# One trunk layer on one core: the first FFN blocks in passes, with their low parts and T sums on VectorE moved

## The chip, the cores and the metric

The kernel runs on one core of a Trainium2 chip. The metric is the device time of one launch in microseconds (us). The core has TensorE for matrix products, VectorE and ScalarE for elementwise work, GpSimd, and SyncE (SP), which issues most loads. Each engine works through its own queue in order, and an instruction that waits holds up everything behind it on its engine.

## The reference

The layer takes x of 512 tokens by 1024 features, all float32:

```
h  = LN(x) * (1 + scale1(c)) + shift1(c)
x1 = LN_1(alpha * x + gate1(c) * HybridMixer(h))          # attention and mLSTM branches, then w_out
h2 = LN(x1) * (1 + scale2(c)) + shift2(c)
out = LN_2(alpha * x1 + gate2(c) * SwiGLU(h2))
SwiGLU(h) = (silu(h @ w_gate) * (h @ w_up)) @ w_down      # 2816 hidden features
```

The change lies between HybridMixer's output projection (w_out), the two normalisations that make h2 from it, and the first of the 22 hidden blocks of 128 features of SwiGLU.

## The kernel before, in words

**Split numbers.** Every matrix operand is kept as a rounded high part and a low part (the value less its high part). The high part is a cast on ScalarE (line 154 for weights, line 178 for activations), the low part a subtraction on VectorE (lines 155 and 179). A product is three matmuls: high by high, high by low, low by high (`mm3`, lines 168 to 175, whose three matmuls have the lines 171, 174 and 175). `POOL_LO` (line 94) names the weights whose low part is subtracted by GpSimd instead: the first piece of the kernel, and the gate and up weights of the FFN blocks 0 and 1.

**Weights.** `emit_chunk` (line 142) loads a weight into a `raw` buffer (a ring of 3; the last two pieces of w_out use the two buffers of the conditioning pool, tag `adaw`), casts it to `whi` and subtracts it to `wlo` (rings of 4). The weights of FFN block 2 go to buffers of their own (`fh`, `fl` in the profile), in the place of two pieces of w_out.

**Output projection and normalisation.** The 512 tokens are 4 tiles of 128. For a tile `wo_seg` makes two halves of 512 features, each 8 slices (`lo4` and `hi4` are the first and last four); `resid1` (line 768) adds the residual and collects statistics; `ln1_a` (line 793) does the first normalisation in place (lines 795, 796) and the second as `xh` (line 799, ScalarE). Each normalisation needs a power -0.5 of the variance, which GpSimd computes (line 195, `lnrs`), and xh a bias (`nmr`, line 200, VectorE). `ln1_b` (line 802) transposes xh on TensorE (8 transposes, line 810, `h2t`), scales it into `h32` (line 815 on ScalarE; for the last tile ScalarE writes the high part and VectorE h32, line 817) and splits it into `hhi` and `hlo` (lines 178 and 179; line 820 for the last tile). The h32 buffers are a ring of 3.

**First FFN blocks.** Blocks 0, 1 and 2 are computed directly: for the first 256 tokens (tiles 0 and 1) gate then up of a block, 8 slices of three matmuls each (lines 911 to 918), with the transposes of tile 2 behind block 0 and those of tile 3 after four slices of block 2; then for the last 256 tokens (lines 923 to 925). The first matmul of each gate or up product is pinned: it stays behind the instruction that the program has before it on TensorE.

**T sums.** The other 19 blocks use seven products in place of eight, with sums of quarter matrices. `build_t` (line 828) makes four sums per pair of tiles from h32 (lines 834 to 837) and splits them into `thi` and `tlo` (lines 839, 840). Its buffers `tt` come from the `raw` ring. `load_pair` (line 897) loads the weights of a block with their sums: one load of 512 KB and three of 256 KB on SP, and two of 256 KB on GpSimd's queue that are added onto what is there (lines 907, 908).

**What sets the order.** A planner fixes the order on each engine when the kernel is built: among instructions that it takes to be ready, the one earlier in the program goes first, and those in a `tc.high_priority()` block go ahead of others. `after(ins, prev)` adds an order edge on one engine, `tc.keep_in_program_order` pins as described. Buffers of a closed pool are reused by the next one once their last reader is done.

Of the kernel before, what the change touches and what calls it, by code (L numbers as in the profile page):

```python
# [16 lines left out]
P = 128  # L17
D = 1024
S = 512
KT = 8  # L20
# [12 lines left out]
CW = 1056  # L33
# [57 lines left out]


PLAN = plan()
POOL_LO = [("start", 0), ("fg", 0), ("fu", 0), ("fg", 1), ("fu", 1)]


@with_exitstack
def block_kernel(ctx, tc, x, c, wada, wpk, cols, gvb, mvb, lnp, out):
    nc = tc.nc
    V, A, G, T = nc.vector, nc.scalar, nc.gpsimd, nc.tensor  # L100
# [26 lines left out]
    stp = ctx.enter_context(tc.tile_pool(name="stp", bufs=4))  # L127
# [5 lines left out]
    st = {"n": 0, "tiles": {}, "resident": {}}  # L133
# [8 lines left out]
    def emit_chunk(i):  # L142
        key = PLAN[i]
        w = chunk_width(key)
        if key in (("wo", 6), ("wo", 7)):
            raw = adap.tile([P, VW], F32, tag="adaw", name=f"raw{i}", bufs=2)
        else:
            raw = stp.tile([P, CW], F32, tag="raw", name=f"raw{i}", bufs=3)
        st["dma"] = nc.sync.dma_start(raw[:, :w], wpk[offs[key]:offs[key] + P * w].rearrange("(p w) -> p w", p=P))
        if key in st["resident"]:  # L150
            hi, lo = st["resident"][key]
        else:
            hi, lo = (stp.tile([P, CS], F32R, tag=t_, name=f"{t_}{i}")[:, w_off(key):w_off(key) + w] for t_ in ("whi", "wlo"))
        st["hi"] = A.copy(hi[:, :w], raw[:, :w])  # L154
        (G if key in POOL_LO else V).tensor_tensor(lo[:, :w], raw[:, :w], hi[:, :w].bitcast(F32), ALU.subtract)  # L155
        st["tiles"][key] = (hi, lo)

    def prefetch(key, ahead):
        i = PLAN.index(key)
# [4 lines left out]
    def get(key, ahead=AHEAD):  # L164
        prefetch(key, ahead)
        return st["tiles"].pop(key)
# [17 lines left out]
    def ln_stats(src):  # L184
        stt = small.tile([P, 2, 6], F32, tag="lnst", name="lnst")
        for h in range(2):
            V.bn_stats(stt[:, h, :], src[:, h * 512:(h + 1) * 512])
        return stt

    def ln_finish(stt):  # L190
# [6 lines left out]

    def nmr(mu_, rs):
        t = small.tile([P, 1], F32, tag="nmr", name="nmr")
        V.tensor_scalar(t, mu_, rs, -1.0, ALU.mult, ALU.mult)  # L200
        return t

    def after(ins, prev):
        tc.add_manual_dep(ins.ins, prev.ins.name, mybir.DependencyInfo(mybir.DependencyClass.NoSync, mybir.DependencyReason.DATA), reason="issue order")
        return ins

    def scope(**kw):
        e = ExitStack()
# [33 lines left out]
    ada_s, adap = scope(name="ada", bufs=2)  # L242
# [83 lines left out]
    for tb in range(TB):  # L326
# [3 lines left out]
        rs = small.tile([P, 1], F32, tag="lnrs", name=f"xrs{tb}")  # L330
# [47 lines left out]
    def hk(k, sl=slice(0, S)):  # L378
        return hhi[:, k, sl], hlo[:, k, sl]
# [330 lines left out]
    for f in range(KT):  # L710
# [4 lines left out]
        hi, lo = get(("pa", f))  # L715
# [21 lines left out]
    for i, c0 in ((0, 16), (1, 40)):  # L737
        pg = tr_tile(f"pg{i}")
# [11 lines left out]
    ln_s, lnq = scope(name="lnq", bufs=1, side="right")  # L750
# [42 lines left out]
    def ln1_a(tb):  # L793
        mu_, rs = ln_finish(zst[tb])
        V.scalar_tensor_tensor(xz[tb], xz[tb], mu_, l1g, ALU.subtract, ALU.mult)
        V.scalar_tensor_tensor(xz[tb], xz[tb], rs, l1b, ALU.mult, ALU.add)
        mu_, rs = ln_finish(ln_stats(xz[tb]))
        xh = lnq.tile([P, D], F32, tag="xh", name=f"xh{tb}")
        A.activation(xh, xz[tb], AF.Identity, bias=nmr(mu_, rs), scale=rs)
        xhs[tb] = xh  # L800

    def ln1_b(tb):
        xh = xhs.pop(tb)
        ts_ = slice(tb * P, (tb + 1) * P)
        h32 = lnq.tile([P, KT, P], F32, tag="h32", name=f"h32{tb}", bufs=3)
        h32s[tb] = h32
        for g in range(2):
            pt = tr_tile(f"h2t{tb}{g}")
            for i in range(4):
                T.transpose(pt[:, i * P:(i + 1) * P], xh[:, (g * 4 + i) * P:(g * 4 + i + 1) * P], ident)  # L810
            for i in range(4):
                d = g * 4 + i
                s_ = slice(i * P, (i + 1) * P)
                sh, sc = mods[:, 32 + d:33 + d], sc2p[:, d:d + 1]
                A.activation(h32[:, d, :] if tb < TB - 1 else hhi[:, d, ts_], pt[:, s_], AF.Identity, bias=sh, scale=sc)
                if tb == TB - 1:
                    V.tensor_scalar(h32[:, d, :], pt[:, s_], sc, sh, ALU.mult, ALU.add)
            if tb == TB - 1:
                ds_ = slice(g * 4, g * 4 + 4)
                V.tensor_tensor(hlo[:, ds_, ts_], h32[:, ds_, :], hhi[:, ds_, ts_].bitcast(F32), ALU.subtract)  # L820
        if tb < TB - 1:
            split(hhi[:, :, ts_], hlo[:, :, ts_], h32)

# [4 lines left out]
    def build_t(a, b):  # L828
        ts_ = slice(a * P, (a + 1) * P)
        b11, b21 = h32s[a][:, 0:4, :], h32s[a][:, 4:8, :]  # L830
        b12, b22 = h32s[b][:, 0:4, :], h32s[b][:, 4:8, :]
        tt = [stp.tile([P, CW], F32, tag="raw", name=f"tt{i}_{a}", bufs=3) for i in range(2)]
        t = [tt[i // 2][:, (i % 2) * S:(i % 2) * S + S].rearrange("p (k t) -> p k t", k=4) for i in range(4)]
        V.tensor_tensor(t[0], b11, b12, ALU.subtract)
        V.scalar_tensor_tensor(t[1], b22, -1.0, t[0], ALU.mult, ALU.subtract)
        V.tensor_tensor(t[2], b22, b12, ALU.subtract)
        V.scalar_tensor_tensor(t[3], b21, -1.0, t[1], ALU.mult, ALU.subtract)
        for i in range(4):
            A.copy(thi[:, i, :, ts_], t[i])
            V.tensor_tensor(tlo[:, i, :, ts_], t[i], thi[:, i, :, ts_].bitcast(F32), ALU.subtract)  # L840

    lo4, hi4, all8 = range(4), range(4, KT), range(KT)
# [20 lines left out]
    ln1_b(1)  # L863
    wo_seg(1, 3, lo4)
    NF0 = 3
    first = []
    for k, key in enumerate((("fg", 2), ("fu", 2))):
        st["resident"][key] = tuple(lnq.tile([P, D], F32R, tag=f"wr{n}{4 + k}", name=f"f{n}{k}") for n in ("h", "l"))
    for f in range(NF0):
        with tc.high_priority():  # L870
            w_ = get(("fg", f), ahead=0), get(("fu", f), ahead=0)
        first.append((*w_, acc2(f"fg{f}"), acc2(f"fu{f}")))
    wo_seg(0, 3, hi4)
    resid1(3, 0, wops[(0, 3)])
    wo_seg(1, 3, hi4)
    resid1(3, 1, wops[(1, 3)])
    ln1_a(3)

    def ffn_mm(ps, w, sl, pin=False, ks_=range(KT)):
        hi, lo = w  # L880
        for k in ks_:
            s_ = slice(k * P, (k + 1) * P)
            mm3(ps[:, sl], (hi[:, s_], lo[:, s_]), hk(k, sl), k == 0, k == KT - 1, pin and k == ks_[0])

    y_s.close()
    ada_s.close()
    tp_s, tp = scope(name="tp", bufs=1)
    thi = tp.tile([P, 4, 4, 256], F32R, name="thi")
    tlo = tp.tile([P, 4, 4, 256], F32R, name="tlo")

    raws = {}

# [4 lines left out]
    def load_pair(f):  # L897
        if f >= FT:
            return
        g = stp.tile([P, CW], F32, tag="raw", name=f"rawg{f}", bufs=3)[:, 0:D]  # L900
        nc.sync.dma_start(g, wpk[offs[("fg", f)]:offs[("fg", f)] + P * D].rearrange("(p w) -> p w", p=P))
        w = tp.tile([P, 3 * S], F32, tag="raw", name=f"raws{f}", bufs=2)
        s1, s3, u2 = (w[:, i * S:(i + 1) * S] for i in range(3))
        for d in (s1, s3):
            nc.sync.dma_start(d, chunk("fu", f, 0))
        nc.sync.dma_start(u2, chunk("fu", f, 1))
        nc.gpsimd.dma_start(s1, chunk("fu", f, 1), accum_op=ALU.add)
        nc.gpsimd.dma_start(s3, chunk("fg", f, 0), accum_op=ALU.add)
        raws[f] = (g, w)

    for f, (wg, wu, pg, pu) in enumerate(first):
        ffn_mm(pg, wg, slice(0, 256), True, lo4)
        if f == 2:
            ln1_b(3)
        ffn_mm(pg, wg, slice(0, 256), True, hi4)
        ffn_mm(pu, wu, slice(0, 256), True)
        if f == 0:
            ln1_b(2)
    build_t(0, 2)
    build_t(1, 3)  # L920
    load_pair(NF0)
    load_pair(NF0 + 1)
    for wg, wu, pg, pu in first:
        ffn_mm(pg, wg, slice(256, 512))
        ffn_mm(pu, wu, slice(256, 512))
# [10 lines left out]
    for f, (_, _, pg, pu) in enumerate(first):  # L936
        t = ftp.tile([P, 7, 256], F32, tag="r", name=f"at{f}", bufs=1).rearrange("p a t -> p (a t)")[:, 0:S]
# [119 lines left out]
    for q in range(4):  # L1057
        pss = [acc2(f"dn{q}{tb}") for tb in range(TB)]
        kl = FT if q < 3 else 8
        for k in range(kl):  # L1060
            if k % 4 == 0:
                w = get(("dn", q * 6 + k // 4))
# [111 lines left out]
```

## Time and profile before

| | us |
|---|---|
| median of 3 runs | 879.7 (879.41 to 880.75) |
| profiled execution | 874.97 |
| its span, first to last instruction | 873.2 |
| TensorE busy in the span | 837.4 (96%) |
| VectorE busy | 597.6 (68%) |
| ScalarE busy | 381.8 (44%) |
| GpSimd busy | 91.8 (11%) |

The profile shows one execution. PE is TensorE's matmuls, PEld its weight loads, DVE VectorE, ACT ScalarE, POOL GpSimd, SP the load queue. Times in rows are from the span's start. A matmul's row shows its own duration; matmuls overlap, so the distance between two starts is what one costs.

### The profile page before, as it was taken

To read this page: it belongs to the slowest core of one execution; us is meant where nothing else is said; L and a number is where in the kernel's file an instruction comes from. 1 tells how busy PE (TensorE), PEld (TensorE's weight loads), DVE (VectorE), ACT (ScalarE), POOL (GpSimd) and SP (SyncE) were. 2 spreads that over 40 slices of the span, in tenths; PEclk is the share of its full clock that TensorE was granted. 3 is DMA by queue.
4 is the path that set the end of the run, shared out by engine and by line. 5 is a ranking of instruction groups with operands and counts; after the bars stand their busy time and mean duration, and the time that the engine had idled before them with its cause. 6 is when DMAs were issued, how large, how long until landed. Compare 5 with 4: busy or idle time off the path is not lost.

```text
span 873.2 us, 14109 instructions
## 1 busy us (share of the span) xinstructions
PE 837.4 (96%) x5510; PEld 750.0 (86%) x5510; DVE 597.6 (68%) x1106; ACT 381.8 (44%) x605; POOL 91.8 (11%) x147
## 2 busy tenths in 40 slices
PE   5999999999989999999999987899999999999996
PEld 3889878777779888888888877899999999999996
DVE  6977546564497658766667796598878887943347
ACT  5555857674454324322222554444444444612110
POOL 4020000000111110000000260012111110000001
PEclk9999999999999999999999998999999999999999
DMA  8962432521221226767784072377777774542212
GB/s 336 350 176 73 141 103 69 138 72 61 97 75 47 90 68 230 259 233 248 261 294 151 1 193 73 102 193 189 179 195 182 171 188 101 173 128 87 98 37 97
DMA packets 46477, 130.08 MB, mean 149 GB/s; under 512 B 5293, under 2 KB 5693, under 8 KB 46410
## 3 DMA queue, kind: packets, MB, share of 16 engines
q1 hardware_dynamic: 37930, 113.97, 38.8%
q0 software_dynamic: 6752, 12.06, 8.1%
q10 hardware_dynamic: 1728, 3.15, 1.2%
q8 instruction: 43, 0.70, 0.3%
q14 instruction: 24, 0.20, 0.1%
HBM read 124.93 MB, written 2.13 MB: 146 GB/s over the span
## 4 chain that ended last, share of the span: by engine, by line
PE 89%; DVE 3%; ACT 1%; issue 1%; DVEq 0%; POOL 0%; ACTq 0%; POOLq 0%
PE p L171 7%; PE p L175 7%; PE p L174 7%; PE dn L171 5%; PE dn L174 5%; PE dn L175 5%; PE mv L171 2%; PE mv L175 2%; PE mv L174 2%; PE mo L171 2%; PE mo L174 2%; PE ga L175 2%; PE gb L175 2%; PE pb L175 2%; PE ga L174 2%; PE gb L171 2%
## 5 line engine op out<-in xcount | busy, mean ns | idle before, releaser
L155 DVE TENSOR_TENSOR wlo<-raw,whi 128x1024 fp32r<-128x1024 f32 (+3 forms) x101 | 112.8, 1120 | 109.7 <-ACT whi L154 102.6
L154 ACT CAST whi<-raw 128x1024 fp32r<-128x1024 f32 (+3 forms) x106 | 102.1, 968 | 183.5 <-PE dn L175 69.1
L174 PE MATMUL dn<-wlo,ah 128*128 128x256 f32 x352 | 96.7, 276 | 0.0
L171 PE MATMUL dn<-whi,ah 128*128 128x256 f32 x352 | 96.6, 276 | 0.0
L175 PE MATMUL dn<-whi,al 128*128 128x256 f32 x352 | 95.5, 276 | 0.0
L171 PE MATMUL p<-thi,whiu 128*128 128x256 f32 x304 | 85.3, 280 | 0.0
L174 PE MATMUL p<-tlo,whiu 128*128 128x256 f32 x304 | 84.9, 279 | 0.0
L175 PE MATMUL p<-thi,wlou 128*128 128x256 f32 x304 | 84.8, 279 | 0.0
L171 PE MATMUL p<-hhi,whiu 128*128 128x256 f32 x228 | 64.5, 283 | 2.8 <-DVE at L939 2.8
L171 PEld LDWEIGHTS dn<-whi,ah 128*128 128x128 f32 x352 | 66.0, 188 | 0.2 <-ACT ah L178 0.2
L174 PEld LDWEIGHTS dn<-wlo,ah 128*128 128x128 f32 x352 | 66.1, 188 | 0.0
L175 PEld LDWEIGHTS dn<-whi,al 128*128 128x128 f32 x352 | 65.3, 188 | 0.0
L174 PE MATMUL p<-hlo,whiu 128*128 128x256 f32 x228 | 64.3, 282 | 0.0
L175 PE MATMUL p<-hhi,wlou 128*128 128x256 f32 x228 | 64.3, 282 | 0.0
L254 DVE CUSTOM_DVE_ANT_0 adaw<-adaw,cb 128x1024 f32<-128x1024 f32 x32 | 39.1, 1223 | 27.6 <-DMA adaw<-in_wada_dram 27.5
L171 PEld LDWEIGHTS p<-thi,whiu 128*128 128x128 f32 x304 | 57.2, 188 | 0.0
L175 PEld LDWEIGHTS p<-thi,wlou 128*128 128x128 f32 x304 | 57.2, 188 | 0.0
L174 PEld LDWEIGHTS p<-tlo,whiu 128*128 128x128 f32 x304 | 57.0, 187 | 0.0
L195 POOL TENSOR_TENSOR lnrs<-lnrs,mhalf 128x1 f32<-128x1 f32 x12 | 12.1, 1007 | 322.4 <-DVE lnrs L194 322.4
L171 PEld LDWEIGHTS p<-hhi,whiu 128*128 128x128 f32 x228 | 43.4, 190 | 3.0 <-issue 3.0
L178 ACT CAST whiu<-raws 128x1024 fp32r<-128x1024 f32 (+1 forms) x38 | 30.8, 834 | 34.1 <-PE p L174 33.9
L175 PEld LDWEIGHTS p<-hhi,wlou 128*128 128x128 f32 x228 | 43.6, 191 | 0.0
(335 smaller groups left out, 2380.4 us busy)
## 6 DMA issues: line engine op xcount, KB each, us to landing
raw<-in_wpk_dram SPq DMA_DIRECT2D x84, 512.0 KB, 3.6
adaw<-in_wada_dram SPq DMA_DIRECT2D x48, 512.0 KB, 4.8
raws<-in_wpk_dram SPq DMA_DIRECT2D x57, 256.0 KB, 3.7
raws<-in_wpk_dram POOLq DMA_DIRECT2D x38, 256.0 KB, 6.4
rawg<-in_wpk_dram SPq DMA_DIRECT2D x19, 512.0 KB, 4.3
raw<-in_wpk_dram SPq DMA_DIRECT2D x16, 256.0 KB, 2.7
raw<-in_wpk_dram SPq DMA_DIRECT2D x8, 384.0 KB, 4.7
raw<-in_wpk_dram SPq DMA_DIRECT2D x4, 528.0 KB, 5.6
```

The costliest lines, as they stand in the source:

```text
L154: st["hi"] = A.copy(hi[:, :w], raw[:, :w])
L155: (G if key in POOL_LO else V).tensor_tensor(lo[:, :w], raw[:, :w], hi[:, :w].bitcast(F32), ALU.subtract)
L171: m = T.matmul(ps, lh, rh, start=first, stop=False)
L174: T.matmul(ps, lh, rl, start=False, stop=False)
L175: T.matmul(ps, ll, rh, start=False, stop=last)
L178: A.copy(hi, src)
L195: G.tensor_tensor(rs, rs, mhalf, ALU.pow)
L254: r_ = V.tensor_tensor_reduce(wt, wt, cb, 1.0, 0.0, ALU.mult, ALU.add, t)
```

## The change

The low parts of the first three blocks' weights (`LATE_LO`) are no longer emitted with the load but collected and emitted later on VectorE by `late_lo`, at places given by the program: one behind tile 3's first part, one after two passes, one ordered behind the last `bn_stats`, one behind the last `nmr`, and the two of block 2 behind it as well. Two of the six weights are loaded into the `adaw` buffers. Five weights, not six, are fetched in the high-priority block.

The first 256 tokens of blocks 0 to 2 are computed in passes: `ffn_pass(f, i)` does one of the three products (0: high by high, 1: weight high by activation low, 2: weight low by activation high) of a block's gate and up, 16 matmuls, and the first matmul of each of the two is pinned.

The T sums get buffers that held w_out, tile 3's h32 another of these, and both `build_t` are ordered behind the last `hlo` on VectorE. The two `load_pair` come ahead of them in the program, and the pool `tp` is opened after the passes.

```diff
-POOL_LO = [("start", 0), ("fg", 0), ("fu", 0), ("fg", 1), ("fu", 1)]
+POOL_LO = [("start", 0)]
+LATE_LO = [(n, f) for f in range(3) for n in ("fg", "fu")]
...
-        if key in (("wo", 6), ("wo", 7)):
+        if key in (("wo", 6), ("wo", 7), ("fu", 1), ("fg", 2)):
             raw = adap.tile([P, VW], F32, tag="adaw", name=f"raw{i}", bufs=2)
...
-        (G if key in POOL_LO else V).tensor_tensor(lo[:, :w], raw[:, :w], hi[:, :w].bitcast(F32), ALU.subtract)
+        if key in LATE_LO:
+            late.append((lo[:, :w], raw[:, :w], hi[:, :w]))
+        else:
+            (G if key in POOL_LO else V).tensor_tensor(lo[:, :w], raw[:, :w], hi[:, :w].bitcast(F32), ALU.subtract)
...
+    def late_lo(n, prev=None):
+        for _ in range(n):
+            lo, raw, hi = late.pop(0)
+            r_ = V.tensor_tensor(lo, raw, hi.bitcast(F32), ALU.subtract)
+            if prev is not None:
+                after(r_, prev)
...
-        h32 = lnq.tile([P, KT, P], F32, tag="h32", name=f"h32{tb}", bufs=3)
+        h32 = lnq.tile([P, KT, P], F32, tag="h32" if tb < 3 else "wrh6", name=f"h32{tb}", bufs=3 if tb < 3 else 1)
...
-        tt = [stp.tile([P, CW], F32, tag="raw", name=f"tt{i}_{a}", bufs=3) for i in range(2)]
+        tt = [lnq.tile([P, D], F32, tag=t_, name=f"tt{t_}_{a}") for t_ in (("wrl6", "wrh7") if a == 0 else ("wrl7", "wrl6"))]
...
+        after(t0, st["hlo3"])
...
-    for f in range(NF0):
-        with tc.high_priority():
-            w_ = get(("fg", f), ahead=0), get(("fu", f), ahead=0)
-        first.append((*w_, acc2(f"fg{f}"), acc2(f"fu{f}")))
+    with tc.high_priority():
+        fw = [get(key, ahead=0) for key in LATE_LO[:5]]
...
     ln1_a(3)
+    late_lo(1)
+    fw.append(get(("fu", 2), ahead=0))
...
-    for f, (wg, wu, pg, pu) in enumerate(first):
-        ffn_mm(pg, wg, slice(0, 256), True, lo4)
-        if f == 2:
-            ln1_b(3)
-        ffn_mm(pg, wg, slice(0, 256), True, hi4)
-        ffn_mm(pu, wu, slice(0, 256), True)
-        if f == 0:
-            ln1_b(2)
+    def ffn_pass(f, i):
+
+        for w, p_ in ((first[f][0], first[f][2]), (first[f][1], first[f][3])):
+            for k in range(KT):
+                m = T.matmul(p_[:, 0:256], w[i // 2][:, k * P:(k + 1) * P], hk(k, slice(0, 256))[i % 2], start=i == 0 and k == 0, stop=i == 2 and k == KT - 1)
+                if k == 0:
+                    tc.keep_in_program_order(m)
+
+    ffn_pass(0, 0)
+    ffn_pass(1, 0)
+    late_lo(1)
+    ffn_pass(0, 1)
+    ln1_b(2)
+    ffn_pass(1, 1)
+    late_lo(1, st["bn"])
+    late_lo(1, st["nmr"])
+    ffn_pass(0, 2)
+    ffn_pass(2, 0)
+    ffn_pass(1, 2)
+    ln1_b(3)
+    late_lo(2, st["nmr"])
+    ffn_pass(2, 1)
+    ffn_pass(2, 2)
+    y_s.close()
+    ada_s.close()
+    tp_s, tp = scope(name="tp", bufs=1)
...
+    load_pair(NF0)
+    load_pair(NF0 + 1)
     build_t(0, 2)
     build_t(1, 3)
-    load_pair(NF0)
-    load_pair(NF0 + 1)
```

## Rows read from the trace of the kernel before

**Rows 1.** The page, busy us of each engine, share of the span, instructions.
```profile
PE 837.4 (96%) x5510; PEld 750.0 (86%) x5510; DVE 597.6 (68%) x1106; ACT 381.8 (44%) x605; POOL 91.8 (11%) x147
```

**Rows 2.** Waits of TensorE: waiting line <- releaser: us in total, times, longest.
```profile
PE h2t L810 <- ACT xh L799: 6.1, 1, 6.1
PE p L171 <- DVE at L939: 2.8, 1, 2.8
...
PE fg L174 <- DVE hlo L179: 2.0, 1, 2.0
```

**Rows 3.** Timeline of TensorE, 504 to 536 us: start, us, instruction, [idle before <-releaser].
```profile
504.56 0.39 PE L175 MATMUL wo<-woh,ylo 128*128 128x512 f32 x1
...
507.06 0.38 PE L174 MATMUL fg<-hlo,whi 128*128 128x256 f32 x1 [1.99 <-DVE hlo L179]
...
514.23 1.03 PE L810 MATMUL h2t<-ident,xh 128*128 128x128 f32 x8
515.02 0.36 PE L171 MATMUL fg<-hhi,whi 128*128 128x256 f32 x1
...
520.75 0.28 PE L171 MATMUL fg<-hhi,fh 128*128 128x256 f32 x1
...
528.45 1.97 PE L810 MATMUL h2t<-ident,xh 128*128 128x128 f32 x8 [6.11 <-ACT xh L799]
...
535.51 0.28 PE L171 MATMUL fg<-hhi,whi 128*128 128x256 f32 x1
```

**Rows 4.** Windows: us, busy us (instructions) by engine, granted clock, DMA share, GB/s.
```profile
246.70:250.20 3.50, 3.46 (x30) 3.46 (x31) 3.07 (x10) 2.99 (x6) 1.12 (x4) 1.00 0.04 15
...
508.50:512.00 3.50, 3.50 (x19) 3.50 (x19) 3.40 (x5) 1.77 (x2) 3.50 (x3) 0.51 0.99 323
...
530.10:532.60 2.50, 2.50 (x14) 2.50 (x13) 1.88 (x5) 1.89 (x5) 0.00 (x0) 0.53 0.00 0
```

**Rows 5.** Timeline of VectorE, 491 to 536 us.
```profile
491.28 0.21 DVE L200 TENSOR_SCALAR nmr<-lnmv,lnrs 128x1 f32<-128x1 f32 x1 [0.66 <-POOL lnrs L195]
491.41 1.21 DVE L179 TENSOR_TENSOR hlo<-h,hhi 128x1024 fp32r<-128x1024 f32 x1
493.20 0.69 DVE L771 TENSOR_TENSOR zt<-wo,g1b 128x512 f32<-128x512 f32 x1 [0.58 <-PE wo L175]
...
500.29 0.15 DVE L194 TENSOR_SCALAR lnrs<-lnmv 128x1 f32<-128x1 f32 x1
502.27 0.69 DVE L771 TENSOR_TENSOR zt<-wo,g1b 128x512 f32<-128x512 f32 x1 [1.82 <-PE wo L175]
...
503.60 3.40 DVE L179 TENSOR_TENSOR hlo<-h,hhi 128x1024 fp32r<-128x1024 f32 x1
...
516.46 0.69 DVE L834 TENSOR_TENSOR tt<-h,h 128x512 f32<-128x512 f32 x1 [1.67 <-ACT h L815]
...
526.90 0.21 DVE L200 TENSOR_SCALAR nmr<-lnmv,lnrs 128x1 f32<-128x1 f32 x1 [0.75 <-POOL lnrs L195]
...
535.26 0.69 DVE L820 TENSOR_TENSOR hlo<-h,hhi 128x512 fp32r<-128x512 f32 x1
```

**Rows 6.** Timeline of GpSimd, 490 to 510 us.
```profile
490.70 0.55 POOL L195 TENSOR_TENSOR lnrs<-lnrs,mhalf 128x1 f32<-128x1 f32 x1 [4.57 <-DVE lnrs L194]
495.92 1.45 POOL L195 TENSOR_TENSOR lnrs<-lnrs,mhalf 128x1 f32<-128x1 f32 x1 [4.67 <-DVE lnrs L194]
...
503.16 6.10 POOL L155 TENSOR_TENSOR wlo<-raw,whi 128x1024 fp32r<-128x1024 f32 x2
```

**Rows 7.** Timeline of ScalarE, 491 to 503 us.
```profile
491.53 1.25 ACT L799 ACTIVATE xh<-xz,nmr,lnrs 128x1024 f32<-128x1024 f32 x1 [0.24 <-DVE nmr L200]
...
499.11 2.98 ACT L154 CAST whi<-raw 128x1024 fp32r<-128x1024 f32 x3
501.95 1.10 ACT L178 CAST hhi<-h 128x1024 fp32r<-128x1024 f32 x1
```

**Rows 8.** DMA issues: tile, queue, count, KB each, median us to landing.
```profile
raw<-in_wpk_dram SPq DMA_DIRECT2D x84, 512.0 KB, 3.6
```

More of the change, by code (lines that the diff above doesn't have):

```diff
@@ L154, in emit_chunk @@
         st["hi"] = A.copy(hi[:, :w], raw[:, :w])
-        (G if key in POOL_LO else V).tensor_tensor(lo[:, :w], raw[:, :w], hi[:, :w].bitcast(F32), ALU.subtract)
+        if key in LATE_LO:
+            late.append((lo[:, :w], raw[:, :w], hi[:, :w]))
+        else:
+            (G if key in POOL_LO else V).tensor_tensor(lo[:, :w], raw[:, :w], hi[:, :w].bitcast(F32), ALU.subtract)
         st["tiles"][key] = (hi, lo)
+    late = []
+    def late_lo(n, prev=None):
[4 more added lines that the diff above has]
+                after(r_, prev)
     def prefetch(key, ahead):
@@ L186, in ln_stats @@
         for h in range(2):
-            V.bn_stats(stt[:, h, :], src[:, h * 512:(h + 1) * 512])
+            st["bn"] = V.bn_stats(stt[:, h, :], src[:, h * 512:(h + 1) * 512])
         return stt
@@ L199, in nmr @@
         t = small.tile([P, 1], F32, tag="nmr", name="nmr")
-        V.tensor_scalar(t, mu_, rs, -1.0, ALU.mult, ALU.mult)
+        st["nmr"] = V.tensor_scalar(t, mu_, rs, -1.0, ALU.mult, ALU.mult)
         return t
@@ L819, in ln1_b @@
                 ds_ = slice(g * 4, g * 4 + 4)
-                V.tensor_tensor(hlo[:, ds_, ts_], h32[:, ds_, :], hhi[:, ds_, ts_].bitcast(F32), ALU.subtract)
+                st["hlo3"] = V.tensor_tensor(hlo[:, ds_, ts_], h32[:, ds_, :], hhi[:, ds_, ts_].bitcast(F32), ALU.subtract)
         if tb < TB - 1:
@@ L831, in build_t @@
         b12, b22 = h32s[b][:, 0:4, :], h32s[b][:, 4:8, :]
-        tt = [stp.tile([P, CW], F32, tag="raw", name=f"tt{i}_{a}", bufs=3) for i in range(2)]
+        tt = [lnq.tile([P, D], F32, tag=t_, name=f"tt{t_}_{a}") for t_ in (("wrl6", "wrh7") if a == 0 else ("wrl7", "wrl6"))]
         t = [tt[i // 2][:, (i % 2) * S:(i % 2) * S + S].rearrange("p (k t) -> p k t", k=4) for i in range(4)]
-        V.tensor_tensor(t[0], b11, b12, ALU.subtract)
+        t0 = V.tensor_tensor(t[0], b11, b12, ALU.subtract)
+        after(t0, st["hlo3"])
         V.scalar_tensor_tensor(t[1], b22, -1.0, t[0], ALU.mult, ALU.subtract)
-        V.tensor_tensor(t[2], b22, b12, ALU.subtract)
+        after(V.tensor_tensor(t[2], b22, b12, ALU.subtract), st["hlo3"])
         V.scalar_tensor_tensor(t[3], b21, -1.0, t[1], ALU.mult, ALU.subtract)
@@ L865, in block_kernel @@
     NF0 = 3
-    first = []
     for k, key in enumerate((("fg", 2), ("fu", 2))):
         st["resident"][key] = tuple(lnq.tile([P, D], F32R, tag=f"wr{n}{4 + k}", name=f"f{n}{k}") for n in ("h", "l"))
-    for f in range(NF0):
-        with tc.high_priority():
-            w_ = get(("fg", f), ahead=0), get(("fu", f), ahead=0)
-        first.append((*w_, acc2(f"fg{f}"), acc2(f"fu{f}")))
+    with tc.high_priority():
+        fw = [get(key, ahead=0) for key in LATE_LO[:5]]
     wo_seg(0, 3, hi4)
@@ L877, in block_kernel @@
     ln1_a(3)
+    late_lo(1)
+    fw.append(get(("fu", 2), ahead=0))
+    first = [(fw[2 * f], fw[2 * f + 1], acc2(f"fg{f}"), acc2(f"fu{f}")) for f in range(NF0)]
     def ffn_mm(ps, w, sl, pin=False, ks_=range(KT)):
@@ L883, in ffn_mm @@
             mm3(ps[:, sl], (hi[:, s_], lo[:, s_]), hk(k, sl), k == 0, k == KT - 1, pin and k == ks_[0])
[L885 to L889, printed above, removed]
     raws = {}
@@ L909, in load_pair @@
         raws[f] = (g, w)
-    for f, (wg, wu, pg, pu) in enumerate(first):
-        ffn_mm(pg, wg, slice(0, 256), True, lo4)
-        if f == 2:
-            ln1_b(3)
-        ffn_mm(pg, wg, slice(0, 256), True, hi4)
-        ffn_mm(pu, wu, slice(0, 256), True)
-        if f == 0:
-            ln1_b(2)
+    def ffn_pass(f, i):
[22 more added lines that the diff above has]
+    tp_s, tp = scope(name="tp", bufs=1)
+    thi = tp.tile([P, 4, 4, 256], F32R, name="thi")
+    tlo = tp.tile([P, 4, 4, 256], F32R, name="tlo")
+    load_pair(NF0)
+    load_pair(NF0 + 1)
     build_t(0, 2)
     build_t(1, 3)
-    load_pair(NF0)
-    load_pair(NF0 + 1)
     for wg, wu, pg, pu in first:
```

## The prediction, on record before the result was known

> **What bounds the kernel now.** The page's busy times come first: TensorE is busy 96% of the span [rows 1], so the time is what TensorE must do plus the holes in it, and a change of order can only win in a hole. The waits of TensorE alone list the holes, longest first [rows 2]: in the stretch that the diff touches there are three, 2.0 us for hlo, 6.1 us for xh and 2.8 us for the first FFN product. The timeline of TensorE places them [rows 3]. The last output projection starts at 504.56 and the next matmul can follow 0.23 us later, at 504.8. The first blocks then run until 535.51, where the second token half begins: 30.7 us for 144 matmuls of 256 columns (three gate and three up blocks, 8 slices, 3 products) and two sets of 8 transposes.
>
> What that work needs without holes: 48 matmuls take 515.02 to 520.75, 0.119 us each; a set of transposes takes 514.23 to 515.02, 0.79 us [rows 3]. So 144 x 0.119 + 2 x 0.79 = 18.8 us. Lost are 30.7 - 18.8 = 11.9 us: 1.99 and 6.11 us of waiting, and 3.8 us left over. The windows show what the 3.8 us are: after each of the two waits the granted clock was 0.51 and 0.53 for a few us, TensorE's lower level (1.2 GHz) [rows 4].
>
> Why the two waits are there is on the other engines. VectorE took 3.40 us for the hlo of tile 1 where the same subtraction of tile 0 took 1.21 [rows 5]; GpSimd ran low parts of weights during all of it [rows 6]. The normalisation of tile 3, which xh needs, has the same neighbour, then the T sums: one of them stood 1.67 us at the head of VectorE's queue waiting for ScalarE at 516.46, and its nmr came only at 526.90 [rows 5].
>
> **The change, part by part.**
>
> *Low parts off GpSimd.* Four GpSimd subtractions go (two of them are the 6.10 us row [rows 6]), so VectorE runs beside an idle GpSimd; four of 1.2 us (hlo of tile 0 has that size, 1.21 [rows 5]) come to VectorE, and the two of the third block, already there, move behind tile 3's nmr. The chain to xh of tile 3, taken from rows that had no such neighbour: tile 2 from zt at 493.20 to the end of lnrs at 500.44 is 7.24 us; then 0.66 us for the power on GpSimd (the wait before nmr at 491.28), 0.25 us from nmr to xh, and 1.25 us of xh [rows 5, 7]: 9.4 us. It starts when the projection ends, at 505.0, so xh is there at 514.4 if nothing is put in between. What is put in between: hlo of tile 1 and of tile 2 and the low parts of three blocks at 1.2 us each, 0 to 6.0 us. VectorE stood idle 1.82 us before 502.27 [rows 5], where one fits for nothing, and two fit into waits for the power. I take 2.5 us: xh at 517.
>
> The row on GpSimd first: the power took 0.55 us with VectorE idle and 1.45 us beside a two-input operation of 128x1024 [rows 6], and the low part put behind the last bn_stats lies beside it, which would make the chain 0.9 us longer. The Trainium skill (GPSIMD Engine Reference, Specifications) says why: the SBUF interfaces are shared, with contention for VectorE instructions that have two SBUF inputs. By that rule an edit that brings two-input work to VectorE makes GpSimd's power slower, and the trace agrees; xh would be at 517.9 by it instead of 517, and the sum is the same, since xh is asked for at 519.0.
>
> *Pass by pass.* The same 144 matmuls come in another order; the count of weight loads equals that of matmuls already (5510 and 5510, [rows 1]), so nothing that was shared is lost.
>
> What the order does: before tile 3's transposes TensorE now has 7 passes of 16 matmuls and tile 2's transposes, 7 x 1.91 + 0.79 = 14.2 us, so it asks for xh at 519.0. Against 517 the 6.11 us wait is gone, with 2 us to spare, and the 2 us of half clock behind it too. The low parts are asked for later: those of block 0 in the fifth pass (504.8 + 3 x 1.91 + 0.79 + 1.91 = 513.2), of block 1 in the seventh (517.1). The first two passes need hhi only, the third hlo of tile 1, at 508.6; so the first wait moves from hlo to hhi.
>
> *That hhi is the weak point.* ScalarE cast three weights one after the other from 499.11, 0.99 us each, before hhi of tile 1, which ended at 503.05 [rows 7]. Now five casts are in the block that goes ahead, with buffers for all of them: four can run at once and end at 503.1. Then hhi alone ends at 504.2, in time. But nmr of tile 2 no longer waits behind GpSimd's subtraction, so xh of tile 2 (1.25 us, earlier in the program) can go before: 505.4, a wait of 0.6 us. If the fifth cast goes before as well: 506.5, 1.7 us. The ends are 0 and 1.7; I take 1.1. For the clock: a 1.99 us wait was followed by 3.5 us at 0.51 [rows 3, 4], a loss of half of it, 1.7; one of 2.42 us, before 246.74, was followed by a full clock [rows 4]. Bounds 0 and 1.7, I take 0.8.
>
> *The second token half* needs hhi and hlo of tile 3. Before, the last hlo ended 7.5 us after the transposes began (528.45 to 535.95 [rows 3, 5]), with transposes at half clock, over 1 us slower, and a T sum in between; I make it 6 us for the last hlo and 5 for the one of its first half. TensorE has 0.79 + 2 passes = 4.6 us of work plus 6 products of high parts (0.7 us): a wait of 0 to 0.7; I take 0.3.
>
> *T sums behind hlo, with own buffers.* 16 VectorE operations (8 sums, 8 low parts) of 128x512, at most 0.69 us each as the last hlo has [rows 5], 11.0 us, now all behind hlo of tile 3, so from about 525 to 536. Their cover is the second token half, 144 x 0.119 = 17.1 us, and the 2.8 us wait behind it: the FFN loop, which reads them, starts at 523.6 + 19.9 = 543.5 at the earliest. No loss; with the cover gone it would be up to 11 us. The buffers (the fourth h32, the sums) lie in output-projection weights last read before 504.8: nothing. The loads of the next two blocks, now later in the program, take space that the projection (until 504.8) and the low parts behind nmr (until about 518) read last; 3.5 MB at the 323 GB/s of [rows 4] are 11 us, done by 529, when block 0's second half (523.6 + 5.7 = 529.3) gives back the first high-part buffer that their casts need: nothing, but see the last rival.
>
> *The 2.8 us wait* before the first FFN product [rows 2] stays: it hangs on silu and multiplication of block 0 (line 939) behind the second half, which nothing here changes.
>
> Sum: 11.9 - 1.1 - 0.8 - 0.3 = 9.7 us. The profiled execution took 874.97 us (span 873.2), 4.7 us below the median 879.7; I carry the saving over unchanged: 879.7 - 9.7 = **870.0**.
>
> **The rivals.**
>
> *A, no wait left.* hhi of tile 1 goes before xh, and the clock holds: 11.9 - 0.3, 868.1. For it: hhi was ready when the casts began; against it: three casts went ahead of it then [rows 7].
>
> *B, VectorE is late.* All low parts but one, both hlo and the slower power go before nmr: xh at 514.4 + 6.0 + 0.9 = 521.3, 2.3 us after 519.0, and up to 2 us of half clock: 9.7 - 4.3 leaves 5.4, 874.3. Against it: idle time at 500.4, and the order written for two of them.
>
> *C, the change is no gain in effect:* xh stays late for something that I don't see (a queue head on ScalarE waiting for the third up block's weights, as VectorE had at 516.46), giving back 5 to 9.7 us: 875 to 879.7.
>
> *D, slower.* The third up block's weights are loaded into the buffer of block 0, free only once its low part is made, and pass (2,0), before tile 3's transposes, needs them. If that low part runs where the program has it, behind nmr of tile 3, at about 514.7, and the two next blocks' loads (each 0.5 MB, three of 0.25 MB and two of 0.25 MB that are added on top; 3.5 MB for two) are ahead of it in SP's queue, these take 11 us at 323 GB/s [rows 4], the load itself 3.6 us [rows 8] less overlap: landed at about 527.5, cast at 528.6, half a pass and one pass to the transposes at 531.5, and 4.6 us to 536.1 instead of 535.51, with 1 to 2 us of half clock: 881.5. It decides from a landing later than about 526. Against it: VectorE's idle time before 502.27 [rows 5] takes the low part, and then the buffer is free before the projection ends.
>
> **Chances.** Forecast (868.8 to 872.5) 0.50; A 0.22; B 0.15; C 0.08; D 0.05. The range takes in A and B with the bounds of their unknown costs: 867.0 to 875.5. What a measurement can tell from no change is about 0.2%, 1.8 us: faster 0.92, within 0.03 (the end of C), slower 0.05.
>
> **What would show it.** Right: TensorE's waits have no xh of tile 3 and no hlo of tile 1; a short wait for hhi of tile 1 at about 505; the passes at 0.119 us a matmul; the second half beginning 20 to 22 us after the projection instead of 30.7; VectorE's hlo of tile 1 at 1.2 us. Wrong: a wait for xh, for a low part or for the third up block's weights inside the passes, or a new wait at the first T product.

## The result: 13.4 us faster, where 9.7 were forecast

| | before | after |
|---|---|---|
| median of the runs | 879.56 us (877.62 to 880.75) | 866.14 us (865.31 to 867.51) |
| profiled execution (span) | 874.97 (873.2) | 867.51 (865.8) |

The ratio is 0.9847 (95%: 0.9828 to 0.9866). The direction was right and the size was not: 866.14 lies 0.9 us under the range. Two slow executions further down, of 1686 us (*after, again*) and of 4719 us (*the passes alone*), are left out of their rows. The page's busy times, which answer to [rows 1]:

```profile
PE 838.6 (97%) x5510; PEld 751.3 (87%) x5510; DVE 595.9 (69%) x1110; ACT 382.1 (44%) x605; POOL 82.8 (10%) x143
```

GpSimd gave up 9 us, VectorE did not grow. The waits of TensorE in the stretch of the change, for [rows 2]: of three, one is left, and it is shorter.

```profile
PE p L184 <- DVE at L968: 1.5, 1, 1.5
```

The timeline of TensorE, for [rows 3]. The projection's last matmul starts at 506.57 and the first pass 0.23 us behind it. Tile 3's transposes (520.82) stand behind a pass with no idle time in brackets, and the second token half begins at 525.53: 18.7 us from 506.80, where 18.8 was the need without holes and 30.7 the time before.

```profile
506.57 0.39 PE L188 MATMUL wo<-woh,ylo 128*128 128x512 f32 x1
506.80 1.10 PE L924 MATMUL fg<-hhi,whi 128*128 128x256 f32 x8
...
519.91 1.07 PE L924 MATMUL fu<-hhi,wlo 128*128 128x256 f32 x8
520.82 1.04 PE L823 MATMUL h2t<-ident,xh 128*128 128x128 f32 x8
...
525.53 0.28 PE L184 MATMUL fg<-hhi,whi 128*128 128x256 f32 x1
...
526.10 0.28 PE L184 MATMUL fu<-hhi,fh 128*128 128x256 f32 x1
526.27 0.38 PE L187 MATMUL fg<-hlo,whi 128*128 128x256 f32 x1
526.49 0.28 PE L188 MATMUL fg<-hhi,wlo 128*128 128x256 f32 x1
...
544.38 0.36 PE L184 MATMUL p<-hhi,whiu 128*128 128x256 f32 x1 [1.50 <-DVE at L968]
```

ScalarE, for [rows 7]: hhi of tile 1 ends at 505.05, 1.75 us before the first pass needs it (506.80), ahead of the fourth and fifth cast and of xh; xh of tile 3 (the row at 516.98) ends at 518.22, 2.6 us before its transposes.

```profile
501.13 2.98 ACT L155 CAST whi<-raw 128x1024 fp32r<-128x1024 f32 x3
503.96 1.09 ACT L191 CAST hhi<-h 128x1024 fp32r<-128x1024 f32 x1
504.91 1.09 ACT L155 CAST whi<-raw 128x1024 fp32r<-128x1024 f32 x1
...
516.98 1.24 ACT L812 ACTIVATE xh<-xz,nmr,lnrs 128x1024 f32<-128x1024 f32 x1
...
538.79 1.28 ACT L967 ACT_TABLE_LOAD   x1 [1.22 <-DVE tlo L854]
542.91 0.60 ACT L967 ACTIVATE at<-fg 128x512 f32<-128x512 f32 x1 [2.84 <-PE fu L188]
```

VectorE, for [rows 5]: hlo of tile 1 takes 1.22 us in place of 3.40, nmr of tile 3 comes 9.7 us after the projection (516.48, against 526.90 less 504.8 = 22.1 before), and the sums (from 526.74) stand behind the last hlo.

```profile
505.31 1.22 DVE L192 TENSOR_TENSOR hlo<-h,hhi 128x1024 fp32r<-128x1024 f32 x1
...
516.48 0.21 DVE L213 TENSOR_SCALAR nmr<-lnmv,lnrs 128x1 f32<-128x1 f32 x1 [0.73 <-POOL lnrs L208]
...
525.53 1.28 DVE L833 TENSOR_TENSOR hlo<-h,hhi 128x512 fp32r<-128x512 f32 x2
526.74 0.68 DVE L847 TENSOR_TENSOR ttwrl<-h,h 128x512 f32<-128x512 f32 x1
```

**The account.** The *stretch* below runs from the projection's end to the first FFN product behind the second half (`p`); the *p stage* from there to the down projection.

| us | before | after | saved |
|---|---|---|---|
| first token half | 30.7 | 18.7 | 12.0 |
| second token half | 16.8 | 17.4 | -0.6 |
| wait before the first FFN product | 2.8 | 1.5 | 1.3 |
| p stage | 189.6 | 188.4 | 1.2 |
| sum | | | 13.9 |

The spans of the two profiled executions differ by 7.4 only: the one of after was 2.0 us late before the stretch began, and its down projection took 124.8 us against 120.3 (last section). 13.9 - 2.0 - 4.5 = 7.4. Two executions of one kernel differ by as much (*after, silu early* was profiled twice, and its projection's last matmul started at 506.88 and at 504.67), so the 2.0 us are not put down to the change.

### The profile page after: what moved, and what is told of

Same layout as the page of the kernel before. It is cut to its first block, busy times and chain, and to the rows that moved or that the text cites. A ratio compares the mean times of both kernels' runs of the same rounds, so it can differ in the third digit from the quotient of the medians.

```text
span 865.8 us, 14110 instructions
## 1 busy us (share of the span) xinstructions
PE 838.6 (97%) x5510; PEld 751.3 (87%) x5510; DVE 595.9 (69%) x1110; ACT 382.1 (44%) x605; POOL 82.8 (10%) x143
## 3 DMA queue, kind: packets, MB, share of 16 engines
q1 hardware_dynamic: 37930, 113.97, 39.1%
## 4 chain that ended last, share of the span: by engine, by line
PE 91%; DVE 1%; ACT 1%; issue 0%; DVEq 0%; ACTq 0%
PE p L187 7%; PE p L184 7%; PE p L188 7%; PE dn L188 5%; PE dn L184 5%; PE dn L187 5%; PE mv L184 2%; PE mv L188 2%; PE mv L187 2%; PE mo L184 2%; PE mo L187 2%; PE ga L184 2%; PE gb L184 2%; PE ga L187 2%; PE gb L187 2%; PE pb L187 2%
## 5 line engine op out<-in xcount | busy, mean ns | idle before, releaser
L267 DVE CUSTOM_DVE_ANT_0 adaw<-adaw,cb 128x1024 f32<-128x1024 f32 x32 | 39.1, 1223 | 27.1 <-DMA adaw<-in_wada_dram 26.9
L191 ACT CAST whiu<-raws 128x1024 fp32r<-128x1024 f32 (+1 forms) x38 | 30.7, 831 | 33.7 <-PE p L187 16.8
L187 PEld LDWEIGHTS p<-hlo,whiu 128*128 128x128 f32 x228 | 42.8, 188 | 0.0
```

Of the source, the lines that this page charges most:

```text
L187: T.matmul(ps, lh, rl, start=False, stop=False)
L191: A.copy(hi, src)
L267: r_ = V.tensor_tensor_reduce(wt, wt, cb, 1.0, 0.0, ALU.mult, ALU.add, t)
```

## The experiments

Twelve runs, each beside runs of the kernel before. The stretch and the p stage are from the profiled execution of each.

| run | median, us | ratio to before (95%) | stretch | p stage |
|---|---|---|---|---|
| before | | | 50.4 | 189.6 |
| the sums alone | 871.76 | 0.9907 (0.988 to 0.9934) | 42.3 | 188.4 |
| the low parts alone | 876.97 | 0.9970 (0.9956 to 0.9984) | 47.2 | 189.6 |
| the passes alone | 878.74 | 0.9981 (0.9962 to 1.0001) | 49.0 | 190.7 |
| after, again | 866.60 | 0.9868 (0.9841 to 0.9895) | 37.6 | 188.4 |
| after, low parts on GpSimd | 867.58 | 0.9850 (0.9808 to 0.9891) | 38.5 | 188.4 |
| after, block order | 867.97 | 0.9867 (0.984 to 0.9894) | 39.1 | 188.4 |
| after, sums not ordered | 870.25 | 0.9890 (0.9861 to 0.9919) | 40.5 | 188.4 |
| after, sums in the raw ring | 867.72 | 0.9884 (0.986 to 0.9907) | 38.9 | 190.8 |
| before, table early | 890.71 | 1.0139 (1.0115 to 1.0164) | 48.9 | 193.1 |
| before, silu early | 873.51 | 0.9927 (0.9901 to 0.9953) | 47.0 | 184.7 |
| after, silu early | 865.04 | 0.9842 (0.9813 to 0.9871) | 35.9 | 187.1 |
| the same, second time | 863.06 | 0.9818 (0.9791 to 0.9844) | 35.9 | 184.7 |

**Taking one part out of after.** First the GpSimd subtractions, which the prediction named first for both waits:

```diff
-POOL_LO = [("start", 0)]
+POOL_LO = [("start", 0), ("fg", 0), ("fu", 0), ("fg", 1), ("fu", 1)]
...
-        if key in LATE_LO:
+        if key in LATE_LO and key not in POOL_LO:
...
-    late_lo(1)
...
-    late_lo(1)
...
-    late_lo(1, st["bn"])
-    late_lo(1, st["nmr"])
```

> The changed kernel with one part undone: the low parts of blocks 0 and 1 are made by GpSimd at load again. Theory 1 (VectorE and GpSimd side by side are what made xh late): hlo of tile 1 takes over 3 us again, the power of tile 3 waits behind GpSimd's subtractions, xh of tile 3 comes 3 to 6 us later than in the changed kernel and TensorE waits for it 1 to 4 us, with some half clock behind it: 869 to 874 us. Theory 2 (the order in passes alone makes the room): no wait in the passes, 866 us, within 1 us of the changed kernel.

VectorE's hlo of tile 1 is slow again, and TensorE hardly notices. VectorE's row, the row of tile 3's xh on ScalarE, and all waits of TensorE but that for `p`:

```profile
504.15 3.44 DVE L192 TENSOR_TENSOR hlo<-h,hhi 128x1024 fp32r<-128x1024 f32 x1
518.24 1.25 ACT L812 ACTIVATE xh<-xz,nmr,lnrs 128x1024 f32<-128x1024 f32 x1 [2.64 <-DVE nmr L213]
```

```profile
PE fg L187 <- DVE hlo L833: 0.6, 1, 0.6
```

xh ends at 519.49, and its transposes start at 519.54. It is 2.7 us later than in after, counted from the projection's end (14.2 against 11.4), which uses up the 2.6 us to spare and no more; the stretch grows by 1.0. The wait for xh that theory 1 expected did not come, and 867.58 lies under its 869 to 874 us. The slowing is real (3.44 against 1.22 us), but it does not by itself explain the 6.1 us wait. The Trainium skill (GPSIMD Engine Reference, Specifications) has GpSimd sharing its SBUF interfaces with VectorE, with contention for VectorE instructions that have two SBUF inputs; the row agrees.

Then the order of the blocks in place of the passes:

```diff
-    ffn_pass(0, 0)
-    ffn_pass(1, 0)
-    late_lo(1)
...
-    ffn_pass(2, 2)
+    late_lo(1)
+    late_lo(1, st["bn"])
+    late_lo(1, st["nmr"])
+    for f, (wg, wu, pg, pu) in enumerate(first):
+        if f == 2:
+            late_lo(2, st["nmr"])
+        ffn_mm(pg, wg, slice(0, 256), True, lo4)
...
```

> The changed kernel with the three products of each slice together again, block after block, and the transposes where they were before; the late low parts stay on VectorE with their order edges. Theory 1 (side by side is the cause): xh of tile 3 is as early as in the changed kernel and not waited for, but block 1's low parts, ordered behind the last bn_stats and nmr, are asked for 2 to 4 us before they are there: 868 to 873 us. Theory 2 (passes make the room): these waits, and half clock behind each, give back over half of the gain: 873 to 878 us. If neither waits: 866 us.

```profile
PE fg L188 <- DVE wlo L167: 1.8, 1, 1.8
```

One wait, for the low part of block 1, because a block asks for its low parts in its first three matmuls; xh is as early as in after (11.4 us after the projection). The time, 867.97, lies at the lower edge of what theory 1 gave. The passes are worth 1.6 us of the stretch here.

Then the order edges of the sums, and their buffers:

```diff
         t0 = V.tensor_tensor(t[0], b11, b12, ALU.subtract)
-        after(t0, st["hlo3"])
...
-        after(V.tensor_tensor(t[2], b22, b12, ALU.subtract), st["hlo3"])
+        V.tensor_tensor(t[2], b22, b12, ALU.subtract)
```

> The changed kernel without the two order edges that keep the T sums behind the last hlo; they keep their own buffers. Theory 1: the sums of tiles 0 and 2 stand ahead of tile 3's chain on VectorE again, 3 to 6 operations of 0.69 us and a wait for ScalarE, so xh comes 2 to 5 us later; TensorE asked for it 2.6 us after it was there, so a wait of 0 to 3 us: 866 to 870 us. Rival (the sums never mattered, GpSimd did): 866 us with no wait and xh no later.

```profile
PE fg L187 <- DVE hlo L833: 2.2, 1, 2.2
PE p L184 <- DVE at L967: 1.5, 1, 1.5
PE fu L923 <- DVE wlo L167: 0.4, 1, 0.4
```

Sums go ahead of the last tile's work on VectorE. xh comes 2.3 us later than in after, as expected, but is still there in time (13.7 us after the projection, asked for at 14.7); the wait comes at hlo of tile 3, which the expectation had not named. The stretch grows by 2.9 us. With the edges kept, but the buffers of before, and the loads behind the sums again:

```diff
-        tt = [lnq.tile([P, D], F32, tag=t_, name=f"tt{t_}_{a}") for t_ in (("wrl6", "wrh7") if a == 0 else ("wrl7", "wrl6"))]
+        tt = [stp.tile([P, CW], F32, tag="raw", name=f"tt{i}_{a}", bufs=3) for i in range(2)]
...
-    load_pair(NF0)
-    load_pair(NF0 + 1)
     build_t(0, 2)
     build_t(1, 3)
+    load_pair(NF0)
+    load_pair(NF0 + 1)
```

> The changed kernel with the T sums' buffers in the raw ring again and the two block loads behind them, the order edges kept. Theory 1 (the own buffers are what moved the table load: silu's output lies over them, so it waits for VectorE as well, and the table load carries only that wait): the table load falls back into the wait, which is 2.8 us again, 867.4 us, or 869 if half clock follows. Rival (the later sums moved it, whatever their buffers): wait of 1.5 us, 866 us.

ScalarE's rows at the end of the second half, then the window behind the wait:

```profile
541.33 1.28 ACT L967 ACT_TABLE_LOAD   x1 [3.41 <-issue]
542.62 0.60 ACT L967 ACTIVATE at<-fg 128x512 f32<-128x512 f32 x1
```

```profile
544.10:551.00 6.90, 6.90 (x35) 6.90 (x36) 5.31 (x8) 4.89 (x8) 0.23 (x1) 0.56 0.57 159
```

The table load is back inside the wait, which is 2.8 us again, and 6.9 us at a clock of 0.56 follow it. This profile carries the explanation of the terms that the prediction left out. It is the slowest of its six executions (869.61 us); the median is 1.1 us above that of after, again, and the intervals overlap, so that the time alone does not show it.

**One part alone in the kernel before.** The sums (own buffers and edges, as in the change):

```diff
-        tt = [stp.tile([P, CW], F32, tag="raw", name=f"tt{i}_{a}", bufs=3) for i in range(2)]
+        tt = [lnq.tile([P, D], F32, tag=t_, name=f"tt{t_}_{a}") for t_ in (("wrl6", "wrh7") if a == 0 else ("wrl7", "wrl6"))]
...
+        after(t0, st["hlo3"])
...
```

> The kernel before with one part of the change alone: T sums in buffers of their own, ordered behind the last hlo on VectorE; low parts, block order and loads as before. Theory 1 (VectorE's queue ahead of tile 3's nmr is what makes xh late, and the sums are its largest avoidable part: four tt and four tlo, about 5 us, and 1.67 us of standing in wait): xh of tile 3 ends 19 us after the projection instead of 23.6, TensorE's wait for it falls from 6.1 to about 1.5 us (0 to 2.5) and the half clock behind it shortens; the 2.0 us wait for hlo of tile 1 stays; 872 to 874. Theory 2 (the sums only fill time in which VectorE would have waited anyway, as in the run with the sums left free): the wait stays above 4 us and the time above 876.

```profile
PE fg L174 <- DVE hlo L179: 2.0, 1, 2.0
PE p L171 <- DVE at L940: 1.5, 1, 1.5
PE h2t L810 <- ACT xh L799: 1.2, 1, 1.2
```

With GpSimd's subtractions and the block order still there, the wait for xh falls from 6.1 to 1.2 us and the one for `p` from 2.8 to 1.5. xh ends 18.7 us after the projection, where theory 1 said 19. This part alone saves 8.0 us in the median, of the 13.4 of the whole change; 871.76 lies 0.2 under theory 1's range of 872 to 874.

The low parts on VectorE alone:

```diff
-POOL_LO = [("start", 0), ("fg", 0), ("fu", 0), ("fg", 1), ("fu", 1)]
+POOL_LO = [("start", 0)]
```

> The kernel before with one part of the change alone: the four low parts of blocks 0 and 1 are made by VectorE at load, block order and T sums as before. Theory 1 (side by side): the 2 us wait for hlo of tile 1 goes, that for xh of tile 3 falls from 6.1 to 2 to 5 us, since the T sums still stand ahead: 871 to 876 us. Theory 2 (order in passes): both waits stay or grow, since VectorE has 4.9 us more to do: 878 to 882 us.

```profile
PE h2t L810 <- ACT xh L799: 5.9, 1, 5.9
PE p L171 <- DVE at L939: 2.8, 1, 2.8
PE fg L174 <- DVE hlo L179: 0.6, 1, 0.6
```

It takes the wait for hlo from 2.0 to 0.6 and leaves that for xh at 5.9, where theory 1 expected 2 to 5; the time, 876.97, lies between the two theories. That is not because xh is as late as before:

```profile
526.08 1.24 ACT L799 ACTIVATE xh<-xz,nmr,lnrs 128x1024 f32<-128x1024 f32 x1 [2.26 <-DVE nmr L200]
527.38 1.97 PE L810 MATMUL h2t<-ident,xh 128*128 128x128 f32 x8 [5.85 <-ACT xh L799]
```

Counted from the projection's end (506.86), xh ends after 20.5 us instead of 23.6. But with the first wait nearly gone TensorE also asks for it 2.9 us earlier, after 14.7 us instead of 17.5. So both ends of the wait moved together, and the 3.2 us of the stretch were won at the first wait and at the clock behind it.

The passes alone (the loop of before replaced by the calls of `ffn_pass`, `ln1_b` between them as in the change, without `late_lo`):

```diff
-    for f, (wg, wu, pg, pu) in enumerate(first):
-        ffn_mm(pg, wg, slice(0, 256), True, lo4)
...
+    ffn_pass(0, 0)
+    ffn_pass(1, 0)
+    ffn_pass(0, 1)
+    ln1_b(2)
...
+    ffn_pass(1, 2)
+    ln1_b(3)
+    ffn_pass(2, 1)
+    ffn_pass(2, 2)
```

> The kernel before with the order of the passes alone; low parts on GpSimd, T sums in the raw ring, loads as before. Theory 1 (the order of TensorE's work only moves the holes as long as VectorE's queue is as long as before): the wait for hlo of tile 1 (2.0 us) goes, xh ends 22 to 23 us after the projection and is asked for at 14.2, so that its wait grows to about 8 us; 877.5 to 879. Theory 2 (the passes carry the gain): xh wait under 4 us, 874 or less.

```profile
510.70 1.09 PE L810 MATMUL h2t<-ident,xh 128*128 128x128 f32 x8 [0.71 <-ACT xh L799]
...
520.46 1.21 PE L915 MATMUL fu<-hhi,fh 128*128 128x256 f32 x8 [1.13 <-ACT fh L154]
...
529.12 1.97 PE L810 MATMUL h2t<-ident,xh 128*128 128x128 f32 x8 [5.57 <-ACT xh L799]
```

The wait for hlo goes, and 7.4 us of waits stand in the place of 8.1. xh of tile 3 ends at 529.07, 22.1 us after the projection (23.6 before), and is asked for 16.5 us after it (17.5 before). Theory 1 had the wait growing to about 8 us; it is 5.57, and two small waits ahead of it are new. No gain that can be told from none.

**The wait before the first FFN product.** A table for silu loaded early was to take 1.3 us off it in the kernel before:

```diff
     build_t(1, 3)
+    dum = small.tile([P, 1], F32, tag="dum", name="dum", bufs=1)
+    A.activation(dum, ones[:, 0:1], AF.Silu)
```

> The kernel before with a silu on one column of ones added behind the T sums, so that the table is loaded before the wait ahead of the first FFN product. Theory 1 (the table load of 1.28 us stood inside that wait, and the change moved it out by accident): the wait falls from 2.8 to 1.5 us: 1.3 us less than before, and 1.7 us more if the clock then holds: 876.5 to 878.3 us. Rival (the wait shrank for another reason): 2.8 us stay, 879.6 us.

This says nothing of the wait: the added activation depends on nothing and ran at the start of the kernel, 2.1 us in, and the projection ended 7.7 us later than in before (why so much is open). The wait of 2.8 us stayed. The better test puts silu and product of blocks 0 and 1 into the second half:

```diff
-    for wg, wu, pg, pu in first:
+    at01 = stp.tile([P, CW], F32, tag="raw", name="at01", bufs=3)
+    for f, (wg, wu, pg, pu) in enumerate(first):
         ffn_mm(pg, wg, slice(256, 512))
         ffn_mm(pu, wu, slice(256, 512))
+        if f < 2:
+            t = at01[:, f * S:(f + 1) * S]
+            A.activation(t, pg, AF.Silu)
+            V.tensor_tensor(t, t, pu, ALU.mult)
...
```

> The kernel before with silu and product of blocks 0 and 1 put into the second token half (buffer from the raw ring); nothing else. Theory 1 (the 2.8 us wait is table load, silu and product behind the second half, and the half clock behind it is its consequence): the wait before the first FFN product goes, from the projection's end to that product 47.5 us instead of 50.3, and the stage behind it 188.4 instead of 189.6; 875 to 876.5. Theory 2 (the wait is hidden by something else that is late, or the clock falls there anyway): a new wait takes its place and the time stays within 1 us of the kernel before.

All waits of TensorE in the stretch:

```profile
PE h2t L810 <- ACT xh L799: 6.1, 1, 6.1
PE fg L174 <- DVE hlo L179: 2.0, 1, 2.0
```

The third is gone and nothing took its place: 3.3 us of stretch and 6.3 us in the median (4.1 to 8.7 by the interval), 1.5 us below theory 1's range. Of these, 3.3 and the 1.2 of the p stage that after also saves are explained; the other 1.8 may be the matmul spacing of the last section, which isn't shown. The same edit on after:

> The changed kernel with silu and product of blocks 0 and 1 written to a buffer of the raw ring, so that they need not wait for the second token half of block 2. If the wait ahead of the first FFN product is only these two steps being late, it goes, 1.5 us less: 864.6 us. Rival (another wait stands behind it: casts or low parts of the first FFN block, or the third buffer of the raw ring is missed by the loads): 866 us or more.

> The changed kernel with silu and product of blocks 0 and 1 in the second token half, a second time. If its lead of 2.3 us over the changed kernel is its own and not the spread of executions: 864 to 866, no wait before the first FFN product; else 866.5 to 867.5.

```profile
531.84 1.28 ACT L958 ACT_TABLE_LOAD   x1
533.13 0.60 ACT L958 ACTIVATE at<-fg 128x512 f32<-128x512 f32 x1
```

Table load and silu lie beside the second half (rows of the first of the two profiles), `p` follows at once, and the medians are 865.04 (864.6 was expected) and 863.06 (864 to 866), the best of all; after had 866.14 and, repeated beside the first of these:

> The changed kernel itself beside the others of this call, for a closer interval: 866 us, 13 us less than before; no half clock within 4 us of the first FFN product. One open point: in the profile of before the matmuls of the down projection are 0.1133 us apart, in that of the changed kernel 0.1177, at full clock in both. If that is a property of the kernels it shows again; if it changes from execution to execution, this profile or those beside it show the other figure for some kernel.

866.60. The profile shows the wait gone both times. The lead over after is 1.6 us where both ran side by side (the expectation of the second run has it as 2.3); their intervals against before overlap, so its size isn't settled.

## Why the prediction was wrong in size

**The three waits and what was lost: right.** 11.9 us of holes in the first half were found, and 12.0 went.

**"*That hhi is the weak point*": this step failed, 1.9 us.** It charged 1.1 us of waiting and 0.8 us of half clock. The cast of hhi kept its place 1.75 us before it was needed, just as before: 503.05 against 504.8 there, 505.05 against 506.80 here. Only three casts went ahead of it, the fourth and fifth followed, and xh of tile 2 came after these. That was rival A, and the first half went its way.

**The 0.3 us for the second half: about half came.** Its first low product (526.27) starts 0.17 us behind the matmul before it, and the next 0.22 us behind that, where 0.12 is the pace: 0.16 us, too short to be listed as a wait. The first of VectorE's two hlo rows (525.53) had ended at 526.21.

**"The 2.8 us wait before the first FFN product stays ... which nothing here changes": this step failed, 2.5 us.** It fell to 1.5, and the half clock behind it went. With the hhi step alone at nothing the forecast would have been 868.1 (rival A); this step is what took the time below the range. The wait is a chain of table load, silu and product. In before, the table load waits for TensorE and lies whole inside it; the rows of ScalarE of before:

```profile
552.38 1.28 ACT L938 ACT_TABLE_LOAD   x1 [9.60 <-PE fu L175]
553.68 0.60 ACT L938 ACTIVATE at<-fg 128x512 f32<-128x512 f32 x1
```

In after, the table load waits for a tlo of VectorE and runs 4.1 us ahead of the activation (538.79), and only the activation waits for TensorE (542.91). The runs tie this to the sums' buffers: with own buffers the wait is 1.5, whether the loads are where they were (*the sums alone*) or the order edges are gone (*sums not ordered*); with the raw ring it is 2.8 in spite of the edges. That silu's buffer lies where the sums were, so that the activation has two waits and the table load takes the one on VectorE, is read from the releasers and not tried by itself. The Trainium skill (ScalarE: Activation LUTs, What ACT_TABLE_LOAD costs) gives about 1283 ns for the load; the rows have 1.28, which is also the 1.3 us won. The 1380 ns of drain that the same place adds show in no row here: the activation starts 1.30 us behind the load (552.38, 553.68). The clock behind the wait, in the first 3.5 us of the p stage, of before:

```profile
555.10:558.60 3.50, 3.46 (x21) 3.49 (x22) 3.08 (x5) 3.37 (x6) 0.00 (x0) 0.68 0.46 147
```

and of after:

```profile
544.40:547.90 3.50, 3.44 (x27) 3.23 (x28) 3.08 (x5) 3.50 (x7) 0.00 (x0) 1.00 0.45 140
```

The other profiles agree: over the 4 us behind a wait of 2.83 us the granted clock was 0.50 to 0.65 (five runs: before, low parts alone, passes alone, raw ring, table early), and behind one of 1.50 us it was 1.00 (six runs). The prediction looked for half clock behind the first two waits and not behind the third.

The two failed steps and the 0.3 us make 4.7; less the 0.6 by which the second half ran longer, 4.1, where 3.7 lie between the forecast saving (9.7) and that of the medians (13.4). Of the 0.6, 0.16 are the late hlo and the rest is the matmul spacing of the last section.

**Why xh was late: half right.** The prediction put it on GpSimd's neighbouring work first and the sums second. The sums are the larger part: moving them alone brings xh 4.9 us forward (23.6 to 18.7 us after the projection) and moving the low parts alone 3.1 (to 20.5); the passes alone bring 1.5. In after, GpSimd's subtractions put back cost 2.7 us of xh, which use up what there is to spare. What made xh late is the work that stands ahead of tile 3's nmr in VectorE's queue. The windows from the projection's end to that nmr, for before, the sums alone and after:

```profile
504.79:526.90 22.11, 19.56 (x25) 0.89 0.66 178
507.18:524.38 17.20, 14.86 (x18) 0.90 1.01 287
506.80:516.48 9.68, 8.34 (x15) 1.00 0.14 45
```

VectorE is busy for most of each: 25 operations in 19.56 us, 18 in 14.86, 15 in 8.34. How long each takes counts too: with GpSimd's subtractions back in after, 15 operations took 11.25 us. The forecast time of xh was right: forecast 12.2 us after the projection (517 against 504.8), measured 11.4; asked for at 14.2, measured 14.0.

**The parts alone** save 8.1, 3.2 and 1.3 us of stretch, 12.6 of the 12.8 together; taken out of after one at a time they cost 1.0 to 2.9, since the 2.6 us to spare for xh cover most of what the missing one costs it (2.7 us without the low parts, 2.3 without the order edges).

**Right as forecast:** no loss by the sums behind hlo, by the loads or by the third up block (rival D): there is no wait for any of them. The power beside a two-input operation took 1.45 us again (at 510.22), the one behind the low part 0.55: that low part ended at 515.44, before the power began at 515.89, so that the 0.9 us did not fall due.

```profile
510.22 1.45 POOL L208 TENSOR_TENSOR lnrs<-lnrs,mhalf 128x1 f32<-128x1 f32 x1 [5.14 <-DVE lnrs L207]
515.89 0.55 POOL L208 TENSOR_TENSOR lnrs<-lnrs,mhalf 128x1 f32<-128x1 f32 x1 [4.21 <-DVE lnrs L207]
```

## What to carry to other kernels

When an operand is late, count what stands ahead of its chain in the queue of the engine that makes it, and move that first; making each operation faster came second here (4.9 us against 3.1). Judge a part by when the operand is ready and not by the wait alone: the wait also shrinks or stays with the time at which it is asked for. A wait that "nothing changes" has parts: follow each instruction of its chain (here a table load) to its own releaser, and ask whether new buffers give it another one. Look at the granted clock behind every wait that shrinks or goes, not only behind the largest.

## What was not expected of the hardware

At a granted clock of 1.00, matmuls of 256 columns come at two spacings. Windows of 40 us, first of before, in the p stage and in the down projection:

```profile
600.00:640.00 40.00, 40.00 (x342) 40.00 (x341) 32.81 (x45) 18.59 (x25) 6.99 (x8) 1.00 0.75 183
760.00:800.00 40.00, 40.00 (x355) 40.00 (x354) 15.57 (x24) 7.97 (x8) 0.00 (x0) 1.00 0.36 113
```

then of before with silu early:

```profile
600.00:640.00 40.00, 40.00 (x355) 40.00 (x354) 33.12 (x46) 18.52 (x26) 7.53 (x9) 1.00 0.76 186
760.00:800.00 40.00, 40.00 (x342) 40.00 (x341) 14.42 (x25) 8.39 (x9) 0.00 (x0) 1.00 0.28 88
```

342 and 355 matmuls, 0.117 and 0.113 us each, in the same code, with the fast stretch at another place. Of the 14 profiled executions one had it in the down projection (120.3 us instead of 124.8), and the three with silu early, and no other, had it for 20 to 90 us behind the place of the wait that they removed. In the second token half it follows the kernel: 96 of the 143 steps are short in before and five more runs (among them after in block order), 4 in after and the six runs of it that keep the passes, 12 in *table early*. What sets it is open; it moves a single execution by up to 4.5 us, so that one profiled time can't stand for a median.
